# Grouped-query attention on one core: K transposed by DMA instead of on PE and DVE, with the order of work planned anew

## The chip, the core and the metric

One core of a Trainium2 chip. The time is that of one execution on the device in microseconds (us). Each execution also has a state: "slow" if it is more than 1.5% above the fastest of the same kernel. Comparisons here are between fast executions unless the text says otherwise.

PE is the matmul engine, PEld its weight load, DVE the vector engine, ACT the scalar engine (exponentials), POOL the general engine, SP the engine that issues most of the DMAs.

## The reference

```python
batch, seq, n_heads, n_kv_heads, dim = 8, 512, 32, 8, 64      # float32
# 4 Q heads share one K/V head; heads first, K and V repeated
scores  = einsum('bhqd,bhkd->bhqk', Q, K) * dim ** -0.5
weights = exp(scores - max(scores)); weights /= sum(weights) + 1e-10
output  = einsum('bhqk,bhkd->bhqd', weights, V)               # back to [b, s, h, d], float32
```

## The kernel before

The work is cut into 32 **units**: one batch times one pair of KV heads, with 8 Q heads. A unit has 16 **score tiles** of [128 keys, 2 heads, 512 queries]. PE writes a tile into one of three PSUM slots. Then 11 tiles go through `Exp` on ACT, and 5 through an exponential made of a multiply-add on DVE (two POOL operations refine one of the five).

```python
def mm_scores(t, slot):                      # a score tile: two 64-row matmuls
    s = spsum.tile([128, 2, S], FP32, name=f"s{slot}")
    ...
        nc.tensor.matmul(s[:, m, :],
            kt[u][64 * m:64 * m + 64, 0 if m == g else 1, kc * 128:(kc + 1) * 128],
            qt[u][64 * m:64 * m + 64, i, :], start=True, stop=True)
```

K and Q must be transposed to [dim, seq]. Both are loaded with a cast to bf16, transposed 128x128 at a time on PE and copied out of PSUM by DVE. K is wanted in two orientations (the pair's heads straight and swapped), and the swapped one is made by two DMAs:

```python
nc.vector.tensor_copy(out=k[:, 0, :], in_=x[:, 0:S])
nc.sync.dma_start(out=k[64:128, 1, :], in_=k[0:64, 0, :])
nc.sync.dma_start(out=k[0:64, 1, :], in_=k[64:128, 0, :])
```

PE's remaining work is cut into **fill pieces**: one output block (four 65-column matmuls, 0.12 us) or one 128x128 transpose (0.06 us). A class `Plan` works through a small timetable and from it fixes the order of instructions on every engine. Four strings and lists steer it: which tiles go to DVE, the order of ACT and DVE tiles, how many fill pieces follow each score tile, and the order of pieces. Each engine is given its instructions in that order.

```python
TILES  = [int(c) for c in "0100010001020100"]
SCORES = "ADAAADAADAADAADA"
FILL   = [0, 0, 8, 0, 0, 6, 9, 0, 0, 8, 0, 0, 12, 0, 0, 9]       # 52 pieces a unit
ORDER  = "K4 o6 o7 08 o7 18 o5 o7".split()                       # K4: four transposes of K
```

The softmax here doesn't subtract the row's maximum and nothing guards it: scores larger than these inputs give would overflow.

Of the kernel before, what the change touches and what calls it, by code (L numbers as in the profile page):

```python
# [10 lines left out]
FP32 = mybir.dt.float32  # L11
# [13 lines left out]
class Plan:  # L25
# [7 lines left out]
    def __init__(self, nu, kind, order, groups, arrive, x_cost, x_behind, fix, nslot, nx, npt):  # L33
# [3 lines left out]
        pt, pair_done, parts = {}, {}, {(0, None): 0.0, (0, 0): 0.0}  # L37
# [5 lines left out]
        carry = 0  # L43

        behind = 0.0

        def run_dve(until):
            nonlocal behind
            while ready:
                j = min(ready, key=lambda j: (max(j[0] - self.dve, 0.0), j[0]))  # L50
                start = max(self.dve, j[0])
                if start > until:
                    return
                ready.remove(j)
                self.ops.append((start, "dve", j[1], j[2]))
                extra = 0.0
                if j[1] != "turn":
                    extra, behind = behind, 0.0
                if j[1] == "score":
                    cost, vis = self.SCH, self.SCH_VIS  # L60
                    slots[j[3]] = start + vis
                    pt[j[2]] = start + vis + (fix if kind(j[2]) == 2 else 0.0)
                else:
                    cost, vis = x_cost(j[2])
                    xs[j[3]] = start + vis
                    if j[1] == "turn":
                        swap = 0.0 if j[2][2] is not None else 3.0 if j[2][1] == 1 else 6.0
                        parts[j[2][1:3]] = start + vis + swap
                    behind += x_behind(j[2])
                self.dve = start + cost + extra  # L70
# [11 lines left out]
        for u in range(nu + 3):  # L82
            scores, fill = order(min(u, nu - 1))
            for k in range(16):
# [32 lines left out]
                loose = u < 1 or u >= nu - 2  # L117
                while carry > 0 and gi < len(groups):
                    f = groups[gi]
                    if f[0] == "skip":  # L120
                        step = min(carry, f[1] - at)
                        carry, at = carry - step, at + step
                        if at == f[1]:
                            gi, at = gi + 1, 0
                        continue
# [30 lines left out]
                    carry -= 1  # L156
                    if at == 0 and f[0] != "close":
                        x = banks[f[2]] = nxt % nx
                        xs[x] = NEVER
                        nxt += 1  # L160
# [8 lines left out]
                carry = min(carry, 16)  # L169
# [6 lines left out]
def kernel(  # L176
# [21 lines left out]
    TILES = [int(c) for c in "0100010001020100"]  # L198
    SCORES = "ADAAADAADAADAADA"
    FILL = [0, 0, 8, 0, 0, 6, 9, 0, 0, 8, 0, 0, 12, 0, 0, 9]  # L200
    ORDER = "K4 o6 o7 08 o7 18 o5 o7".split()
    LAST_TILES = [int(c) for c in "0000200011010010"]
    LAST = {
        NU - 2: ("ADADAADAAAADADAA", [0, 0, 15, 32, 32, 0, 0, 0, 24, 0, 0, 0, 0, 0, 32, 3]),
        NU - 1: ("DAADAADDAAAADAAA", [1, 32, 0, 7, 1, 0, 7, 0, 0, 0, 0, 1, 0, 20, 32, 9]),
    }
    SKIP = 22
# [10 lines left out]
    kn_pool = ctx.enter_context(tc.tile_pool(name="kn", bufs=2))  # L218
# [3 lines left out]
    kt_pool = ctx.enter_context(tc.tile_pool(name="kt", bufs=4))  # L222
    pa_pool = ctx.enter_context(tc.tile_pool(name="pa", bufs=17))
    pd_pool = ctx.enter_context(tc.tile_pool(name="pd", bufs=7))
    lo_pool = ctx.enter_context(tc.tile_pool(name="lo", bufs=3))
    two_pool = ctx.enter_context(tc.tile_pool(name="two", bufs=2))
    raw_pool = ctx.enter_context(tc.tile_pool(name="raw", bufs=3))
# [5 lines left out]
    qn, kn, vn, v1 = {}, {}, {}, {}  # L233
    qt, kt = {}, {}
# [15 lines left out]
    def load_k(b):  # L250
        t = kn_pool.tile([128, SC, KV * D], BF16, name="k_nat")
        nc.gpsimd.dma_start(out=t, in_=rows(K, b, 0, KV))
        kn[b] = t
# [15 lines left out]
    def mm_scores(t, slot):  # L269
        p, kc = divmod(t, SC)  # L270
        u, i = divmod(p, HPG)
        s = spsum.tile([128, 2, S], FP32, name=f"s{slot}")
        g = 2 * i // HPG
        for m in range(2):
            nc.tensor.matmul(  # L275
                s[:, m, :],
                kt[u][64 * m:64 * m + 64, 0 if m == g else 1, kc * 128:(kc + 1) * 128],
                qt[u][64 * m:64 * m + 64, i, :],
                start=True,
                stop=True,  # L280
            )
        score[t] = s
# [15 lines left out]
    def exp_dve(t):  # L298
        two = tile_kind(t) == 2
        pts[t] = (two_pool if two else pd_pool).tile(  # L300
# [42 lines left out]
    def take_out(f, now):  # L343
# [6 lines left out]
        if last and lo >= 2 * BLK:  # L350
            divide(u, lo, n, nc.vector, x[:, 0:n * D1].rearrange("p (n c) -> p n c", c=D1))
            if lo == 2 * BLK + 4:
                store(u, 2 * BLK, BLK, nc.sync)
            elif lo >= 3 * BLK:
                store(u, lo, n, nc.scalar if lo == 3 * BLK else nc.sync)
            return
# [38 lines left out]
    def mm_turn(f, at):  # L395
        _, u, part, _ = f
        if at == 0:
            xs[f] = xpsum.tile([128, 2048], U8, name="x").bitcast(BF16)
        i, sc = divmod(at, SC)
        if part is None:  # L400
            src = kn[u // GP][:, sc, 128 * (u % GP):128 * (u % GP + 1)]
        else:
            j = 2 * part + i
            src = qn[u][:, sc, 128 * j:128 * (j + 1)]
        nc.tensor.transpose(xs[f][:, at * 128:(at + 1) * 128], src, ident)  # L405

    def take_turn(f):
        _, u, part, _ = f
        x = xs.pop(f)
        if part is None:  # L410
            k = kt_pool.tile([128, 2, S], BF16, name="kt")
# [3 lines left out]
            kt[u] = k  # L415
# [8 lines left out]
    def tile_kind(t):  # L424
        return (LAST_TILES if t >= 16 * (NU - 1) else TILES)[t % 16]

    turned = {}
    groups = [("skip", 2), ("turn", 0, 1, 8), ("skip", 4), ("turn", 1, None, 4)]
    groups += [("skip", SKIP - 6), ("turn", 1, 0, 8), ("turn", 1, 1, 8)]
    for u in range(NU - 1):  # L430
        lo = 0
        for word in ORDER:
            kind, n = word[0], int(word[1:])
            if kind == "o":
                groups.append(("out", u, lo, n))
                lo += n
            elif u + 2 < NU:
                groups.append(("turn", u + 2, None if kind == "K" else int(kind), n))
# [16 lines left out]
    def arrive(f):  # L455
        return {(0, 1): 0.5, (1, None): 3.0}.get(f[1:3], 6.0 if f[1] == 1 else 0.0)

    plan = Plan(
        NU, tile_kind, lambda u: LAST.get(u, (SCORES, FILL)), groups, arrive, x_cost, x_behind,
        fix=6.0, nslot=NSLOT, nx=2, npt=6,  # L460
    )

    with tc.manual_schedule(engines={PE, ACT, DVE, POOL, SP}):
        q32 = first.tile([128, SC, HPG * D], FP32, name="q32")
        k32 = first.tile([128, SC, 2 * D], FP32, name="k32")
        v32 = first.tile([128, SC, 2 * D], FP32, name="v32")
        q16 = first.tile([128, SC, HPG * D], BF16, name="q16")
        k16 = first.tile([128, SC, 2, 2 * D], BF16, name="k16")
        warm = first.tile([128, S], BF16, name="warm")
        nc.sync.dma_start(out=k32, in_=rows(K, 0, 0, 2))  # L470
        nc.scalar.dma_start(out=q32[:, :, 0:2 * D], in_=rows(Q, 0, 0, 2))
        nc.sync.dma_start(out=q32[:, :, 2 * D:4 * D], in_=rows(Q, 0, 2, 4))
# [10 lines left out]
        load_k(0)  # L483
        load_q(1)

# [4 lines left out]
        nc.vector.tensor_copy(out=k16[:, :, 0, :], in_=k32)  # L490
        nc.vector.tensor_copy(out=k16[:, :, 1, 0:D], in_=k32[:, :, D:2 * D])
        nc.vector.tensor_copy(out=k16[:, :, 1, D:2 * D], in_=k32[:, :, 0:D])
        nc.scalar.copy(out=q16[:, :, 0:2 * D], in_=q32[:, :, 0:2 * D])
        kt[0] = kt_pool.tile([128, 2, S], BF16, name="kt")
        qt[0] = qt_pool.tile([128, HPG, S], BF16, name="qt")

        def turn_first(src, copy, dst):
            x = xpsum.tile([128, 2048], U8, name="x").bitcast(BF16)
            for sc in range(SC):
                nc.tensor.transpose(x[:, sc * 128:(sc + 1) * 128], src[:, sc, :], ident)  # L500
            copy(out=dst, in_=x[:, 0:S])

        turn_first(k16[:, :, 0, :], nc.vector.tensor_copy, kt[0][:, 0, :])
        turn_first(q16[:, :, 0:2 * D], nc.scalar.copy, qt[0][:, 0, :])
        turn_first(k16[:, :, 1, :], nc.vector.tensor_copy, kt[0][:, 1, :])
        nc.vector.tensor_copy(out=q16[:, :, 2 * D:4 * D], in_=q32[:, :, 2 * D:4 * D])
# [3 lines left out]
        load_v(0)  # L510
# [3 lines left out]
        pending_first = True  # L514
        due = False
        for now, engine, what_kind, what in plan.ops:
# [6 lines left out]
            elif engine == "pe":  # L523
                b, r = divmod(what[0], 16 * GP)
                if r == 24 and b + 1 < B:
                    load_k(b + 1)
                    load_v(b + 1)
# [3 lines left out]
                if pending_first and what[0] > 0:  # L531
                    pending_first = False
                    turn_first(q16[:, :, 2 * D:4 * D], nc.vector.tensor_copy, qt[0][:, 1, :])
# [41 lines left out]
```

## Time and profile before

| | before |
|---|---|
| time, median | 350.9 us |
| span in the profile | 349.2 us |
| first exponential on ACT | 7.90 us |
| units 0 and 1 together | 20.76 us |
| a steady unit (median of units 6 to 28) | 10.34 us |
| last exponential to the end | 7.0 us |

The unit times are distances between starts of ACT's exponentials (every eleventh) in the trace's records. From the page of the kernel before: the busy time of each engine, then the chain of waits by engine and by line, then the two large DMA queues.

```profile
PE 336.7 (96%) x5774; PEld 224.5 (64%) x5774; DVE 329.1 (94%) x463; ACT 333.7 (96%) x356; POOL 280.2 (80%) x201
...
PE 48%; ACT 38%; POOL 5%; DVE 3%; issue 3%; DMA 1%; POOLq 0%; ACTq 0%
...
q0 software_dynamic: 25344, 24.91, 47.5%
q1 hardware_dynamic: 25552, 38.28, 32.3%
```

Three engines are at 94 to 96%, and no one of them holds the chain alone: PE has 48% of it, ACT 38%. The DMA queues have 80% of the engines' time.

The timeline of ACT in the kernel before. Columns: start, length, engine, line, operation, number; in brackets the idle time before it and its releaser. The first two lines are the start, the third is a piece from the middle.

```profile
7.90 10.19 ACT L288 ACTIVATE pa<-s 128x1024 bf16<-128x1024 f32 x11 [0.75 <-PE s L275]
18.32 15.95 ACT L288 ACTIVATE pa<-s 128x1024 bf16<-128x1024 f32 x17 [0.23 <-PE s L275]
...
79.42 100.60 ACT L288 ACTIVATE pa<-s 128x1024 bf16<-128x1024 f32 x107
```

The third line says "no idle for 100 us", yet the pace is readable: (100.60 - 1.02) / 106 = 0.939 us from start to start, while exponentials whose input is ready start 0.904 us apart. One exponential is 1.02 us long and the next starts 0.904 us after it, so the two overlap; a wait shorter than this overlap does not count as idle.

### The profile page before, as it was taken

Reading aid. Unit: us, or ns where it says so; the run is one execution under the profiler, and the core shown is the slowest. Engines: PE = TensorE matmul, PEld = TensorE weight load, DVE = VectorE, ACT = ScalarE, POOL = GpSimd, SP = SyncE. Lnnn points to the kernel's source line nnn. Section 1 sums busy time; section 2 is a strip of 40 time slices with the busy share of each in tenths; the row PEclk is TensorE's granted clock in tenths of the full one; section 3 lists DMA queues with packets and bytes.
Section 4 is the critical chain, followed back from the end, with each engine's and each line's share of the span. In section 5 each row is a group of like instructions: output and inputs, shape, how many; then the busy total and the mean of one; then the engine's idle time right before and its main releaser. Section 6 shows DMA issues by size and latency. Waiting matters only on the chain.

```text
span 349.2 us, 12952 instructions
## 1 busy us (share of the span) xinstructions
PE 336.7 (96%) x5774; PEld 224.5 (64%) x5774; DVE 329.1 (94%) x463; ACT 333.7 (96%) x356; POOL 280.2 (80%) x201
## 2 busy tenths in 40 slices
PE   8799999999999999999999999999999999999992
PEld 3366666666666666666666666666666666666661
DVE  3899999999999999999999999999999999999982
ACT  3999999999999999999999999999999999999981
POOL 6369797879978797987978889787997879787692
PEclk9999999999999999999999999999999999999997
DMA  8999567898669958698786986799765996823337
GB/s 184 208 156 181 160 174 196 192 203 200 164 161 237 263 115 207 141 237 222 196 198 140 215 198 168 194 198 224 170 171 163 234 259 129 208 86 137 122 141 223
DMA packets 52008, 64.40 MB, mean 184 GB/s; under 512 B 3441, under 2 KB 36593, under 8 KB 51953
## 3 DMA queue, kind: packets, MB, share of 16 engines
q0 software_dynamic: 25344, 24.91, 47.5%
q1 hardware_dynamic: 25552, 38.28, 32.3%
q8 instruction: 45, 0.74, 0.8%
q10 hardware_dynamic: 1056, 0.39, 0.4%
q14 instruction: 11, 0.08, 0.1%
HBM read 50.86 MB, written 33.55 MB: 242 GB/s over the span
## 4 chain that ended last, share of the span: by engine, by line
PE 48%; ACT 38%; POOL 5%; DVE 3%; issue 3%; DMA 1%; POOLq 0%; ACTq 0%
ACT pa L288 38%; PE s L275 21%; PE x L334 19%; PE x L405 6%; POOL o_sb L378 3%; DMA kt<-kt 1%; DVE pd L305 1%; PE x L488 1%; POOL sum L321 1%; POOL hi L315 1%; DVE raw L357 1%; DVE qt L419 1%; PE x L500 0%; DVE lo L305 0%; POOLq L570 0%
## 5 line engine op out<-in xcount | busy, mean ns | idle before, releaser
L288 ACT ACTIVATE pa<-s 128x1024 bf16<-128x1024 f32 x353 | 331.2, 1027 | 3.9 <-PE s L275 3.3
L275 PE MATMUL s<-qt,kt 64*128 64x512 bf16 x1024 | 163.1, 381 | 4.3 <-ACT pa L288 1.4
L305 DVE TENSOR_SCALAR pd<-s 128x1024 uint16<-128x1024 f32 x128 | 155.9, 1218 | 2.0 <-PE s L275 2.0
L334 PEld LDWEIGHTS <-pa 128*128 128x128 bf16 x2816 | 135.8, 97 | 29.2 <-issue 29.0
L334 PE MATMUL x<-v,pa 128*128 128x65 bf16 x2728 | 150.6, 194 | 0.2
L334 PE MATMUL x<-v,pd 128*128 128x65 bf16 x992 | 131.8, 194 | 0.2 <-DVE raw L357 0.2
L378 POOL TENSOR_TENSOR o_sb<-raw,inv 128x1024 f32<-128x1024 f32 (+1 forms) x64 | 118.7, 1880 | 1.7 <-DVE inv L373 1.3
L275 PEld LDWEIGHTS <-kt 64*128 64x128 bf16 x1024 | 55.8, 93 | 68.5 <-issue 37.8
L334 PEld LDWEIGHTS <-pd 128*128 128x128 bf16 x1024 | 98.8, 98 | 0.4 <-issue 0.2
L357 DVE COPY raw<-x 128x455 f32<-128x455 f32 (+3 forms) x159 | 91.8, 579 | 4.7 <-PE x L334 4.1
L315 POOL TENSOR_TENSOR hi<-lo,shift 128x512 int32<-128x512 int32 x32 | 40.6, 1268 | 49.3 <-PE x L334 37.6
L321 POOL TENSOR_TENSOR sum<-lo,hi 128x1024 bf16<-128x1024 bf16 x32 | 68.0, 2125 | 2.5
L405 PE MATMUL x<-ident,q_nat 128*128 128x128 bf16 x504 | 43.6, 220 | 0.0
L419 DVE COPY qt<-x 128x1024 bf16<-128x1024 bf16 x63 | 42.8, 680 | 0.0
L305 DVE TENSOR_SCALAR lo<-s 128x1024 uint16<-128x1024 f32 x32 | 39.1, 1222 | 0.5 <-PE s L275 0.5
L405 PEld LDWEIGHTS <-q_nat 128*128 128x128 bf16 x504 | 29.9, 98 | 7.7 <-issue 7.7
L334 PE MATMUL x<-v,sum 128*128 128x65 bf16 x248 | 34.7, 194 | 0.0
L245 POOL DMA_DIRECT2D q_nat<-in_Q_dram x32 | 25.5, 797 | 0.0
L334 PEld LDWEIGHTS <-sum 128*128 128x128 bf16 x256 | 25.0, 98 | 0.2 <-issue 0.2
L263 POOL COPY v<-v_nat 128x2048 bf16<-128x2048 bf16 x8 | 15.2, 1905 | 5.7 <-DMA v_nat<-in_V_dram 5.7
L405 PE MATMUL x<-ident,k_nat 128*128 128x128 bf16 x124 | 17.3, 222 | 0.0
L405 PEld LDWEIGHTS <-k_nat 128*128 128x128 bf16 x124 | 7.5, 98 | 7.1 <-issue 7.1
(35 smaller groups left out, 66.7 us busy)
## 6 DMA issues: line engine op xcount, KB each, us to landing
out_dram<-o_sb SPq DMA_DIRECT2D x30, 1024.0 KB, 5.3
q_nat<-in_Q_dram POOLq DMA_DIRECT2D x31, 512.0 KB, 5.9
k_nat<-in_K_dram POOLq DMA_DIRECT2D x8, 512.0 KB, 8.8
v_nat<-in_V_dram POOLq DMA_DIRECT2D x8, 512.0 KB, 10.8
kt<-kt SPq DMA_DIRECT2D x62, 64.0 KB, 5.1
out_dram<-o_sb SPq DMA_DIRECT2D x2, 512.0 KB, 3.8
out_dram<-o_sb SPq DMA_DIRECT2D x3, 256.0 KB, 3.9
q<-in_Q_dram ACTq DMA_DIRECT2D x1, 256.0 KB, 4.5
```

Source lines behind the costliest of these rows:

```text
L245: nc.gpsimd.dma_start(out=t[:, :, lo * D:], in_=rows(Q, b, HU * gp + lo, HU * (gp + 1)))
L263: nc.gpsimd.tensor_copy(out=t[:, :, :, 0:D], in_=vn.pop(b).rearrange("p sc (h d) -> p sc h d", h=KV))
L275: nc.tensor.matmul(s[:, m, :], kt[u][64 * m:64 * m + 64, 0 if m == g else 1, kc * 128:(kc + 1) * 128], qt[u][64 * m:64 * m + 64, i, :], st ...
L288: recent.append(nc.scalar.activation(out=pts[t][:, ms, :], in_=src[:, ms, :], func=mybir.ActivationFunctionType.Exp, scale=float(scale),))
L305: nc.vector.tensor_scalar(out=bits, in0=score.pop(t), scalar1=float(A_schr), scalar2=float(B_two if two else B_one), op0=mybir.AluOpType.mult,
L315: nc.gpsimd.tensor_tensor(out=high.rearrange("p m s -> p (m s)").bitcast(I32), in0=bits.rearrange("p m s -> p (m s)").bitcast(I32), in1=shift,
L321: nc.gpsimd.tensor_tensor(out=dst, in0=bits.bitcast(BF16), in1=high.bitcast(BF16), op=mybir.AluOpType.add)
L334: nc.tensor.matmul(xs[f][:, at * D1:(at + 1) * D1], pts[(u * HPG + i) * SC + kc][:, m, qc * 128:(qc + 1) * 128], v1[u][:, kc, 2 * i // HPG ...
L357: nc.vector.tensor_copy(out=raws[u][:, lo:lo + n, :], in_=x[:, 0:n * D1])
L378: eng.tensor_tensor(out=osbs[u].rearrange("p qc h d -> p h qc d")[:, lo // SC + h0:lo // SC + h0 + nh], in0=src[:, :, 0:D].rearrange("p (h ...
L405: nc.tensor.transpose(xs[f][:, at * 128:(at + 1) * 128], src, ident)
L419: nc.vector.tensor_copy(out=qt[u][:, 2 * part:2 * part + 2, :], in_=x)
```

## The change

Its intent: take K of batches 1 to 7 off PE and DVE. A casting DMA puts K as bf16 into DRAM, one DMA transpose brings a batch's K into SBUF, two DMAs make the swapped orientation. The freed time is to be used by a new order. The first tiles' loads are cut smaller. More output work is done in units 0 and 1, so that the end has less to catch up. The diff, cut to its core:

```diff
+    def load_k(b):
+        ks[b] = ks_pool.tile([S, KV * D + 64], BF16, name="ks")[:, 0:KV * D]        # DRAM
+        nc.gpsimd.dma_start(out=ks[b], in_=K[b].rearrange("s h d -> s (h d)"))
+    def turn_k(b):
+        straight[b] = kt_pool.tile([128, GP, S], BF16, name="straight")
+        nc.sync.dma_start_transpose(out=straight[b], in_=ks.pop(b))
+    def swap_k(b):
+        t = straight.pop(b)
+        k = kt_pool.tile([128, GP, S], BF16, name="swapped")
+        nc.sync.dma_start(out=k[0:64], in_=t[64:128])
+        nc.sync.dma_start(out=k[64:128], in_=t[0:64])
 ...
+    rank = {t: i - (early + 0.5 if kind(t) == 2 else 0.0) for i, t in enumerate(qd)}   # two-step tiles earlier
 ...
-    TILES = [int(c) for c in "0100010001020100"]
-    FILL = [0, 0, 8, 0, 0, 6, 9, 0, 0, 8, 0, 0, 12, 0, 0, 9]
-    ORDER = "K4 o6 o7 08 o7 18 o5 o7".split()
+    TILES = [int(c) for c in "0100020100010001"]
+    FILL = [0, 0, 7, 0, 0, 7, 0, 0, 7, 0, 0, 7, 0, 10, 0, 10]
+    ORDER = "o6 18 08 o7 o7 o7 o5".split()
+    ORDER_FIRST = "o7 K4 18 o5 08 o7 o7 o6".split()
+    EARLY = 3
+    HEAD = 114                                    # pieces done before unit 2; and own orders for 4 units
 ...
+    load, turn, swap = (24, 40, 52) if n == 1 else (64 * n - 80, 64 * n - 52, 64 * n - 26)   # tile numbers
 ...
-        nc.sync.dma_start(out=k32, in_=rows(K, 0, 0, 2))
-        nc.scalar.dma_start(out=q32[:, :, 0:2 * D], in_=rows(Q, 0, 0, 2))
-        nc.sync.dma_start(out=q32[:, :, 2 * D:4 * D], in_=rows(Q, 0, 2, 4))
+        nc.sync.dma_start(out=k32[:, 0:1], in_=rows(K, 0, 0, 2)[:, 0:1])
+        nc.scalar.dma_start(out=q32[:, 0:half], in_=rows(Q, 0, 0, 2)[:, 0:half])
+        nc.sync.dma_start(out=k32[:, 1:SC], in_=rows(K, 0, 0, 2)[:, 1:SC])
+        nc.scalar.dma_start(out=q32[:, half:SC], in_=rows(Q, 0, 0, 2)[:, half:SC])
+        nc.sync.dma_start(out=q32b, in_=rows(Q, 0, 2, 4))
```

## The prediction

> **What bounds the kernel now.** The page shows three engines full at once: PE 96%, ACT 96%, DVE 94% of 349.2 us. The starts of ACT's exponentials in the trace split this. From unit 1 to unit 29 (a unit is 16 score tiles, 11 on ACT, 5 on DVE) one unit takes 10.34 us. Back-to-back exponentials start 0.904 us apart, so ACT alone needs 11 x 0.905 = 9.96. (The Trainium skill, "ScalarE: Activation LUTs", section "What ACT_TABLE_LOAD costs", gives 186 + 0.833 x 1024 - 93 = 946 ns; the trace's 0.904 decides.) The other 0.38 us are waits of about 0.1, three or four a unit: pitches of 1.0 to 1.07 us, the exponential starting 0.04 after a score matmul ended. Summed start to start, DVE needs 5 x 1.141 (exponentials) + 2.58 (five output evictions) + 2 x 0.597 (Q) + 0.278 (K) + 0.26 (reciprocal) = 10.0. PE needs about 9.8: scores 16 x 0.222, outputs 32 x 0.123, 20 transposes x 0.057, some 0.1 per switch. All three lie within 5% of 10.34, coupled by three score slots; the coupling costs the rest.
>
> Outside the steady part: the first exponential starts at 7.90 us (K lands 4.8, Q 5.25, then cast, transposes, evictions); the last two units take 11.25 and 12.02, since PE then catches up on outputs that lag about a unit; the last exponential ends at 342.2, the last store 7.0 later.
>
> **What changes.** For batches 1 to 7, K's transposes leave PE (0.23 us a unit) and its eviction leaves DVE (0.278 a unit). They become a casting DRAM-to-DRAM load, a DMA transpose and two half-swaps a batch. DVE falls to 9.74, PE to about 9.6; ACT stays 9.96 and becomes the longest. Exponentials per unit stay 11 and 5. The first inputs are cut smaller; K's orientations for units 0 and 1 are made on chip. 114 fill pieces precede unit 2 (about 80 now), so outputs lag half a unit less and the tail has less to catch up.
>
> The transpose moves 512 KB a batch. The Trainium skill, "DMA: Bandwidth & Descriptors", section "Latency and other measured facts", gives 261 GB/s: an estimate of 2 us; no trace of before shows one. At least 24 tiles lie between its steps (12 for batch 1), so I expect it hidden.
>
> **Sum (estimates).**
> - Steady part: 10.34 to 10.07 (most of the coupling goes), 28 units: -7.6 us.
> - First exponential at 6.7: -1.2.
> - Units 0 and 1 carry more fills: +0.3.
> - Last two units 23.3 to 20.9: -2.4.
> - After the last exponential: -0.1.
>
> 350.9 - 11.0 = 339.9 us. Range 336.5 to 344.0. Faster by over 2% (below 343.9) 0.80, within 2% 0.17, slower 0.03.
>
> **What would show it.** Steady unit near 10.0 to 10.1, ACT at 98%, DVE idle about 3%; in the chain of waits ACT's exponential well over its 38%; fewer than one pitch over 1.0 us a unit; first exponential before 7 us; last two units under 10.6 each; PE transposes down by about 112, K evictions by 28.
>
> **What would make it wrong.** The steady unit stays above 10.2, because the score slots and not the sums set it. K of batch 1 lands late and PE stalls near 45 us. Transposes hold the sync queue and delay stores, or fill the DMA engines (already about 80% busy), so that Q lands late. Early fills starve ACT in the first two units.

## The result, and the profile after

Twelve executions of the changed kernel gave a median of 355.7 us, from 345.9 to 476.7. Eight were slow: six between 355.2 and 360.2 us, and two at 418.0 and 476.7 us. The four fast ones were 345.9 to 348.8 us, a ratio to the fast executions of before of 0.990 (interval 0.988 to 0.992). Fourteen executions of the kernel before in the same rounds were all within 350.6 to 351.4. A ratio here is the mean time of one kernel's fast executions over that of the other's in the same rounds, so it is not quite the ratio of the medians quoted.

The profile fell on the slowest execution. From its page: busy times, the clock granted to PE in 40 slices (tenths of full speed), and the chain of waits.

```profile
PE 467.7 (98%) x5666; PEld 277.4 (58%) x5666; DVE 331.3 (70%) x436; ACT 345.0 (73%) x356; POOL 280.8 (59%) x205
...
PEclk7555555555555555555555555555555555555555
...
PE 96%; DMA 2%; ACT 1%; POOL 0%; issue 0%; DVE 0%; POOLq 0%; DVEq 0%
```

PE had 0.555 of its clock from 4.15 us to 471.8 us and was the bound. This says nothing about the change's design. The same kernel was run again (a1_again), and its profile fell on a fast execution: busy times, chain, DMA queues.

```profile
PE 333.3 (97%) x5666; PEld 220.3 (64%) x5666; DVE 322.6 (94%) x436; ACT 329.8 (96%) x356; POOL 280.9 (82%) x205
...
ACT 66%; PE 22%; DVE 3%; issue 3%; DMA 2%; POOL 2%; DVEq 0%; POOLq 0%; ACTq 0%
...
q1 hardware_dynamic: 36080, 41.55, 45.4%
q0 software_dynamic: 25872, 24.78, 44.7%
```

ACT now holds 66% of the chain, as intended, and the DMA queues take 90% of the engines' time for 80% before. ACT's timeline of the same execution, the start and a piece from the middle:

```profile
7.39 1.94 ACT L310 ACTIVATE pa<-s 128x1024 bf16<-128x1024 f32 x2 [1.66 <-PE s L297]
9.95 1.02 ACT L310 ACTIVATE pa<-s 128x1024 bf16<-128x1024 f32 x1 [0.62 <-PE s L297]
11.30 6.60 ACT L310 ACTIVATE pa<-s 128x1024 bf16<-128x1024 f32 x7 [0.32 <-PE s L297]
18.63 1.94 ACT L310 ACTIVATE pa<-s 128x1024 bf16<-128x1024 f32 x2 [0.73 <-PE s L297]
21.16 1.94 ACT L310 ACTIVATE pa<-s 128x1024 bf16<-128x1024 f32 x2 [0.59 <-PE s L297]
23.32 1.94 ACT L310 ACTIVATE pa<-s 128x1024 bf16<-128x1024 f32 x2 [0.22 <-PE s L297]
25.61 8.85 ACT L310 ACTIVATE pa<-s 128x1024 bf16<-128x1024 f32 x9 [0.35 <-PE s L297]
...
79.79 101.14 ACT L310 ACTIVATE pa<-s 128x1024 bf16<-128x1024 f32 x109
```

In the middle the pace is (101.14 - 1.02) / 108 = 0.927 us for 0.939: better, but not 0.904. In the start ACT stops six times between 9 and 26 us where it stopped once before.

Where the time went, between the two fast traces (all from the starts of exponentials; the spans are 349.2 and 344.2 us):

| stretch | before | after, fast | difference | predicted |
|---|---|---|---|---|
| to the first exponential | 7.90 | 7.39 | -0.5 | -1.2 |
| units 0 and 1 | 20.76 | 24.09 | +3.3 | +0.3 |
| units 2 to 29 | 289.7 | 285.9 | -3.8 | -7.6 |
| units 30 and 31 | 23.9 | 22.1 | -1.8 | -2.4 |
| last exponential to the end | 7.0 | 4.7 | -2.3 | -0.1 |
| sum | 349.2 | 344.2 | -5.0 | -11.0 |

Two questions remain: why a fast execution is 6 us slower than predicted, and what the slow ones are.

### The profile page after: what moved, and what is told of

Read it like the earlier page. It is cut to its first block, busy times and chain, and to the rows that moved or that the text cites. A ratio compares the mean times of both kernels' runs of the same rounds, so it can differ in the third digit from the quotient of the medians.

```text
span 474.9 us, 12653 instructions
## 1 busy us (share of the span) xinstructions
PE 467.7 (98%) x5666; PEld 277.4 (58%) x5666; DVE 331.3 (70%) x436; ACT 345.0 (73%) x356; POOL 280.8 (59%) x205
## 4 chain that ended last, share of the span: by engine, by line
PE 96%; DMA 2%; ACT 1%; POOL 0%; issue 0%; DVE 0%; POOLq 0%; DVEq 0%
PE x L356 44%; PE s L297 42%; PE x L428 11%; DMA q_nat<-in_Q_dram 2%; ACT pa L310 1%; DVE o_sb L401 0%; DVE inv L396 0%; POOL shift L511 0%; POOL ident masks.py:199 0%; POOL ident masks.py:197 0%; POOL v1f L508 0%; POOLq masks.py:199 0%; DVEq L396 0%; POOLq L623 0%
## 5 line engine op out<-in xcount | busy, mean ns | idle before, releaser
L310 ACT ACTIVATE pa<-s 128x1024 bf16<-128x1024 f32 x353 | 342.9, 1019 | 121.4 <-PE s L297 121.1
L356 PEld LDWEIGHTS <-pa 128*128 128x128 bf16 x2816 | 188.7, 117 | 93.9 <-issue 93.2
L356 PE MATMUL x<-v,pa 128*128 128x65 bf16 x2728 | 207.6, 222 | 0.0
L356 PE MATMUL x<-v,pd 128*128 128x65 bf16 x992 | 192.2, 234 | 0.0
L297 PE MATMUL s<-qt,swapped 64*128 64x512 bf16 x448 | 188.3, 539 | 0.1
L297 PE MATMUL s<-qt,straight 64*128 64x512 bf16 x448 | 188.4, 536 | 0.0
L337 POOL TENSOR_TENSOR hi<-lo,shift 128x512 int32<-128x512 int32 x32 | 40.4, 1262 | 167.4 <-DVE lo L327 167.3
L356 PE MATMUL x<-v,sum 128*128 128x65 bf16 x248 | 49.3, 240 | 0.0
L297 PEld LDWEIGHTS <-swapped 64*128 64x128 bf16 x448 | 34.6, 106 | 21.8 <-issue 10.6
L297 PEld LDWEIGHTS <-straight 64*128 64x128 bf16 x448 | 34.5, 106 | 18.8 <-issue 6.4
L297 PE MATMUL s<-qt,kt 64*128 64x512 bf16 x96 | 21.5, 528 | 1.3 <-DVE qt L536 0.8
```

The source lines that it names most:

```text
L297: nc.tensor.matmul(s[:, m, :], kt[u][int(m != g) if u > 1 else g][64 * m:64 * m + 64, kc * 128:(kc + 1) * 128], qt[u][64 * m:64 * m + 64, ...
L310: recent.append(nc.scalar.activation(out=pts[t][:, ms, :], in_=src[:, ms, :], func=mybir.ActivationFunctionType.Exp, scale=float(scale),))
L337: nc.gpsimd.tensor_tensor(out=high.rearrange("p m s -> p (m s)").bitcast(I32), in0=bits.rearrange("p m s -> p (m s)").bitcast(I32), in1=shift,
L356: nc.tensor.matmul(xs[f][:, at * D1:(at + 1) * D1], pts[(u * HPG + i) * SC + kc][:, m, qc * 128:(qc + 1) * 128], v1[u][:, kc, 2 * i // HPG ...
```

## The experiments

Theories for the slow executions: **A**, the new start uses PE too thinly and the clock gate misbehaves; **B**, a limiter answers to the denser steady part; **C** and later **K**, the DMA transpose, or rather K of batch 1 coming late. For the steady unit: **E**, the sum of work on an engine sets it; **L**, a loop through ACT, a score slot and PE's in-order fill chunk sets it.

### First round: the kernel again, its two halves, a longer warm-up

a1_again: no edit.

> The changed kernel once more, to have a trace of a fast execution and more executions to count. Theory A (the start: the clock gate does not open cleanly with the new start) expects that slow executions differ from fast ones by the clock alone, from the first microseconds on, and that a fast one has steady units of about 10.05 to 10.2 us. Theory B (a limiter answers to the denser steady part) expects the granted clock to fall only once the steady part runs, in stretches in the middle. Fast executions about 346 us, slow ones 354 to 480, about half of all.

Measured: fast at 345.4 to 347.7 us (ratio 0.987, interval 0.985 to 0.989), 2 of 6 slow (355.3 and 355.5 us at clocks 0.989 and 0.982). The steady unit is 10.18 us.

a2_konly: the kernel before, with K by DMA and, from unit 3 on, four pieces fewer in the fill list. Core of the edit:

```diff
+    FILL2 = [0, 0, 7, 0, 0, 5, 8, 0, 0, 7, 0, 0, 12, 0, 0, 9]
-            elif u + 2 < NU:
+            elif u + 2 < (GP if kind == "K" else NU):
-                    load_k(b + 1)
+                    ...  # send_k, turn_k, swap_k at the changed kernel's tile numbers
```

> The kernel before with one part of the change alone: K of batches 1 to 7 by casting load, DMA transpose and swaps; start, tile order and tail as before. Theory A (start) expects every execution at full clock, as before, and a time of 347 to 349 us if the steady unit falls a little (PE and DVE have 0.25 us less per unit). Theory B (denser steady part) expects slow executions here too. If the DMA transpose itself costs, this is slower than before at full clock.

Measured: 363.3 us, **3.5% slower than before** (1.034 to 1.037), all four executions fast, clock 0.990 to 0.996. The steady unit rose from 10.34 to 10.70 us although PE and DVE have less to do. ACT's timeline in it:

```profile
86.93 10.49 ACT L311 ACTIVATE pa<-s 128x1024 bf16<-128x1024 f32 x11 [0.19 <-PE s L298]
97.62 10.52 ACT L311 ACTIVATE pa<-s 128x1024 bf16<-128x1024 f32 x11 [0.19 <-PE s L298]
```

The hoped-for 347 to 349 us did not come; of what was expected, only "slower than before at full clock" did, which would blame the DMA transpose. The changed kernel has the same transposes and a unit of 10.18 us, so they alone do not cost this. It is a first blow to theory E: work was removed and the unit grew. That my four removed pieces had shifted the rest against the score tiles is likely, but no run shows it by itself. K of batch 1 was in time here: 4.3 us before its first use in the trace.

a3_nokdma: the changed kernel, with K of batches 1 to 7 on PE again: `K4` in `ORDER`, and `FILL = [0, 0, 8, 0, 0, 8, 0, 0, 8, 0, 0, 8, 0, 10, 0, 10]`.

> The changed kernel with K of batches 1 to 7 turned on PE again (one 4-block group a unit, eviction on DVE, swaps by DMA); new start, orders and tail stay. Theory A (start) expects slow executions at low clock here as well, about as often; theory B (density from the freed PE and DVE) expects none. Fast executions: steady unit back at about 10.3 us, so 347 to 350 us.

Measured: 380.2 us (ratio 1.083), 5 of 5 fast, steady unit 11.42 us, not 10.3. The order that I gave it was bad, so it does not tell what K's work costs on PE. It has the changed kernel's start and no slow execution, which speaks against theory A, though its trace does have 3.4 us at half clock, from 9.5 us on.

a4_warm16: `for _ in range(16):` in place of 10.

> The changed kernel with 16 warm-up matmuls instead of 10: PE is busy without a break for about 7 us instead of 4.3. Theory A (start) expects the slow executions to become rare or vanish, with fast ones within 1.5 us of those of the changed kernel (first exponential up to 1.5 us later). Theory B expects slow executions as often as without.

Measured: 2 of 6 slow (354.4, 357.5 us); fast ones 345.5 to 348.1. Theory A falls back further. In its trace the first exponential came 1.6 us later than in a1_again, yet unit 2 began at 31.4 us as there (31.5): something later in units 0 and 1 than the first exponential sets their end.

### Second round: density, the transpose, the fill chunk, one load

b1_dense: seven 512-column matmuls around the transposes that wait for the second pair of Q heads.

```diff
                 if scored == 3:
+                    fill_pe(5)
                     turn_first_q(1)
+                    fill_pe(2)
```

> The changed kernel with seven idle-filling matmuls of 512 columns in the start, where PE waits for the second pair of Q heads. Theory A (PE is too thinly used in the first 15 us, and the clock gate[...] closes or opens late) expects slow executions to vanish (0 of about 6, where the changed kernel had 10 of 18), fast time within 1 us of the changed kernel's. Theory B (limiter answers to a dense steady part) and theory C (the DMA transpose or a late K) expect slow ones as often as before.

Measured: 1 of 4 slow (354.6 us). Theory A's cure doesn't cure.

b2_plain: the transpose replaced by a plain DMA; the result is wrong.

```diff
-        nc.sync.dma_start_transpose(out=straight[b], in_=ks.pop(b))
+        nc.sync.dma_start(out=straight[b], in_=ks.pop(b).rearrange("(g p) s -> p g s", p=128))
```

> The changed kernel with the DMA transpose replaced by a plain DMA of the same 512 KB into the same tile; the result is wrong on purpose. Theory C (transpose engages or delays something) expects no slow executions, and if the transpose burdens the steady part, a unit below 10.18 us. Theories A and B expect slow executions in about half of the runs and the same steady unit of 10.18 us: then the transpose is free.

Measured: 345.9 us, 4 of 4 fast, steady unit 10.18 us. The transpose burdens the steady part no more than a plain DMA of the same bytes. From issue to landing the plain DMA took 9.6 to 10.3 us, the transpose of the same 512 KB 9.9 to 11.6 us in a1_again. It is about as slow as the loads of its size here (median 7.9 to 10.6 us in a1_again), and not the estimated 2 us. The issues with their median time to landing, in a1_again and then in b2_plain, and PE's wait for the swapped K of batch 1 in b2_plain:

```profile
straight<-ks SPq DMA_TRANSPOSE x7, 10.7
...
straight<-ks SPq DMA_DIRECT2D x7, 512.0 KB, 10.1
...
PE s L297 <- DMA swapped<-straight: 0.3, 1, 0.3
```

So K of batch 1 was not in time here either, and its wait of 0.3 us cost little: unit 3 took 10.9 us. Four fast executions do not free the transpose of blame, nor do they convict it.

b3_detune: the same 48 pieces a unit, placed otherwise.

```diff
-    FILL = [0, 0, 7, 0, 0, 7, 0, 0, 7, 0, 0, 7, 0, 10, 0, 10]
+    FILL = [0, 0, 9, 0, 0, 6, 0, 0, 7, 0, 0, 6, 0, 10, 0, 10]
```

> The changed kernel with the same 48 fill pieces a unit in other places: 9, 6, 7, 6, 10, 10 between the scores instead of 7, 7, 7, 7, 10, 10. Not one instruction more or less. Theory L (the steady unit is a loop: an exponential ends, PE scores the freed slot, does the whole fill chunk, scores the next tile, whose exponential may then start) expects about 10.4 us a unit, some 7 us more in all; theory E (engine sums set it) expects 10.18. For the slow state: theory B (density of the steady part) expects none or few, as the unit is slower than before's 10.34; theory A expects about half.

Measured: 362.7 us, all at clocks of 0.974 to 0.984. The steady unit is 10.41 us. ACT's timeline:

```profile
106.98 10.24 ACT L310 ACTIVATE pa<-s 128x1024 bf16<-128x1024 f32 x11 [0.17 <-PE s L297]
117.40 10.23 ACT L310 ACTIVATE pa<-s 128x1024 bf16<-128x1024 f32 x11 [0.17 <-PE s L297]
127.80 10.23 ACT L310 ACTIVATE pa<-s 128x1024 bf16<-128x1024 f32 x11 [0.17 <-PE s L297]
```

Each unit of 11 exponentials now ends in a visible stop of 0.17 us, and the units start 10.42 and 10.40 us apart, with not one instruction more or less than the changed kernel. This agrees with theory L, which had said 10.4 (from the kernel's own timetable arithmetic), against theory E, which had said no change. The slower units are not the whole difference to a1_again: much of the rest is a single unit of 21.4 us, taken up in the third round. The low clocks of all five suggest that all have it; then all count as fast by the rule, though none is undisturbed.

b4_q32b: `nc.scalar.dma_start(out=q32b, ...)` for `nc.sync.dma_start(out=q32b, ...)`.

> The changed kernel with one line moved: the load of the second pair of Q heads is issued by ACT behind the first pair instead of third on the sync queue. It landed at 7.99 us and the first unit waited for it. Expected: lands near 6.5 to 7, units 0 and 1 together 23 us instead of 24.1, total 1 us less in fast executions; if theory A holds, somewhat fewer slow executions.

Measured: 348.1 us (ratio 0.991), worse. The load landed at 9.55 us, later than on the sync queue, where it landed between 5.4 and 8.2 us in the traces of nine runs; unit 0 took 14.9 us and the clock was at half for 6.8 us in it, from 10.6 us on. A miss: another issuing engine did not make this load faster. None of its 5 executions was slow. So half clock in the start, which theory A fears, does occur, but the execution with it took 348.1 us, not 354.

### Third round: K of batch 1

b3_detune's trace had shown, besides its slower unit, one unit of 21.4 us: PE waited 8.3 us for the swapped K of batch 1, since its order had put a store ahead of the swap on the sync queue, and the clock was at half for 10.2 us, from 4 us into that wait on. In the fast trace of the changed kernel the same data comes only just in time. The timeline of the sync queue in a1_again (start, time on the queue, line, what is moved), then in a second fence, from PE's timeline of the same execution, its first matmul on the swapped K of batch 1:

```profile
31.19 0.39 SPq L413 DMA_DIRECT2D out_dram<-o_sb  x1
31.68 5.73 SPq L267 DMA_TRANSPOSE straight<-ks  x1
41.61 0.47 SPq L272 DMA_DIRECT2D swapped<-straight  x1
42.13 0.59 SPq L273 DMA_DIRECT2D swapped<-straight  x1
45.96 0.40 SPq L413 DMA_DIRECT2D out_dram<-o_sb  x1
```

```profile
47.19 0.38 PE L297 MATMUL s<-qt,swapped 64*128 64x512 bf16 x1
```

The load lands at 31.58 us, the transpose at 41.60, the second swap at 45.84: a margin of 1.35 us. Right behind the swap comes a 1 MB store. If the chain were 2 us later, the swap would share the DMA engines with that store. First use is at 47.2 us, well before unit 4 begins (its first exponential is at 52.0), because `EARLY` pulls a two-step DVE tile forward.

c0_again: no edit, as the base on the same chip.

> The changed kernel once more, as the base on the same chip for the next three. Over all runs so far 10 of 18 were slow. Theory K (K of batch 1 is late: in fast traces its swapped half landed at 45.8 us and was first used at 47.2, a margin of 1.35 us, and right behind it the sync queue starts a 1 MB store) expects slow executions again, between one and four of six, about 8 to 9 us longer.

Measured: 2 of 6 slow (354.5, 358.0 us); the ratio of the fast ones is 0.988 (0.984 to 0.992).

c1_early: `(16, 32, 44) if n == 1` for `(24, 40, 52)`.

> The changed kernel with the chain of K of batch 1 (load, transpose, swap) issued 8 tiles earlier, one line. Theory K expects no slow execution in six and fast ones at the changed kernel's fast times (346 to 347), give or take 1 us for loads that compete in the start. Theories A (clock gate in the start by itself) and B (dense steady part) expect slow ones as often as in the base.

Measured: 345.7 us, 4 of 4 fast, ratio 0.985 (0.983 to 0.987). The load itself moved by only 0.4 us (POOL reached it at 22.8 us), but the transpose now stands before the store and landed at 38.2 us. Its swap then ran beside the end of the store (to 40.4 us) and a load of Q (to 45.8 us) and took 8.4 us, so the margin was 0.6 us in this trace, less than in a1_again, and unit 3 took 10.7 us for 10.2. No execution was slow, but four are few.

c2_late: `(27, 40, 52) if n == 1`.

> The same chain pushed the other way: the load of K of batch 1 issued 3 tiles (about 2 us) later, transpose and swap at the same places. Theory K expects every execution slow, 353 to 358 us, with a wait of PE for the swapped K of some 3 to 7 us near 47 us in the trace, the granted clock at half for one to three windows after it, and unit 3 at 18 to 20 us instead of 10.2. Theories A and B expect no change from the base.

Measured: 347.9 to 355.0 us, median 353.0. By the 1.5% rule three count as slow, but five of the six are at a clock of 0.989 or 0.990 and 351.6 us or more; one escaped. The load was issued at 34.4 us, 11 us later and not 2, because its place in POOL's order came after other work. From its trace, of a slow execution: the waits between 40 and 60 us (engine, line, releaser; total, times, longest), then PE and its clock in 40 slices.

```profile
ACT pa L310 <- PE s L297: 8.2, 2, 7.0
...
PE s L297 <- DMA swapped<-straight: 6.8, 1, 6.8
```

```profile
PE   7799938999999999999999999999999999999994
...
PEclk9999996999999999999999999999999999999999
```

PE waits 6.8 us for the swapped K (47.43 to 54.19). The granted clock is at half for 6.83 us (51.63 to 58.46), 4.3 us of it after the wait. Unit 3 takes 19.0 us for 10.2. The Trainium skill, "TensorE: Matmul & The Clock Gate", section "Part 1: The HAM clock gate (the "warmup" mystery)", says that the gate goes to half clock after an idle window of about 3.4 us. The traces agree in the lengths, 6.83 us here and 10.24 us in b3_detune, two and three times 3.413; and PE was idle for the whole 3.4 us before the drop in both. But a full window of idleness was not needed: in d2_best, below, PE was busy for 46% of the 3.4 us before the drop. So a late K costs its wait and then a stretch at half clock: 8.8 us in all here.

c3_split: transpose and swap of each batch cut in two, the first KV pair's quarter first.

```diff
+        nc.sync.dma_start_transpose(out=t[:, 0:1], in_=ks[b][:, 0:128])
+        nc.sync.dma_start(out=k[0:64, 0], in_=t[64:128, 0])
+        nc.sync.dma_start(out=k[64:128, 0], in_=t[0:64, 0])
+        nc.sync.dma_start_transpose(out=t[:, 1:GP], in_=ks.pop(b)[:, 128:])
```

> The changed kernel with each batch's transpose and swap cut in two: the first pair of KV heads (a quarter of the bytes) first, the other three behind it. Theory K expects K of the first unit of batch 1 to land at about 38 to 40 us, a margin of over 6 us, so no slow execution, and fast ones as in the base.

Measured: 346.2 us, 4 of 4 fast, within 0.5 us of each other, ratio 0.986 (0.985 to 0.988). The first quarter landed, swapped, at 41.1 us, later than the 38 to 40 expected, with a margin of 6.4 us.

### Fourth round: the start, and a better version

In c3_split's trace PE waits 0.8 us, until 19.7 us, for Q of unit 2, a load that POOL issues only at 11.9 us, after casts that wait for other loads.

d1_loadq: c3_split, with that load issued before the casts.

```diff
+        load_q(2)
         load_k_pairs(2, 2)
         load_v(0)
 ...
-        load_q(2)
         load_q(3)
```

> The split version (no slow executions) with one more line moved: the load of Q for unit 2 is issued by POOL before its casts of the first tile, which wait for other loads, instead of after them. In the split version it was issued at 11.9 us, landed at 19.7 and PE waited 0.8 us for it, and ACT with it. If the waits for Q set units 0 and 1 (12.6 and 12.1 us), unit 1 falls by 0.8 to 1.5 us and the total to about 345; if the larger number of fill pieces before unit 2 sets them, little changes.

Measured: units 0 and 1 fell from 24.8 to 23.6 us, but 3 of 6 executions were slow (351.9 to 358.4 us). The trace is a slow one: the first quarter's transpose, issued at 33.2 us, landed at 45.4, PE waited 5.7 us for the swapped K, unit 3 took 17.8 us and the clock was at half for 6.8 us. The sync queue and PE's wait:

```profile
30.52 0.40 SPq L420 DMA_DIRECT2D out_dram<-o_sb  x1
33.16 1.60 SPq L273 DMA_TRANSPOSE straight<-ks  x1
45.41 0.47 SPq L274 DMA_DIRECT2D swapped<-straight  x1
...
PE s L304 <- DMA swapped<-straight: 5.7, 1, 5.7
```

Splitting the chain did not make it safe: a quarter took 12 us here and 6 in c3_split. It was not the transpose alone: the store issued at 30.5 us took 11.8 us to land (6.2 in c3_split), and the load of Q at 33.9 us 11.7 (5.8). Why all transfers were slow at that time is not known.

d2_best: d1_loadq with measured arrivals in the timetable and other orders for units 0, 1 and the steady part.

> As the one before, with the order of work planned again for the loads' measured arrivals in the first two units, and a steady order of fill pieces and exponentials (fill 7, 7, 7, 7, 11, 9, other DVE tiles) that the loop theory puts at 10.13 us a unit for 10.17. Expected: steady unit 10.13 to 10.15, last two units 0.3 less, units 0 and 1 together 22.5 to 24, no slow execution, total 343 to 345 us, so faster than both kernels. If engine sums set the steady unit, it stays at 10.18 us.

Measured: 353.1 us (ratio 1.005), a failure in every point but one. The steady unit is 10.17 us, so the 10.13 that the loop account promised did not come; K was late twice in the trace (of the slowest execution, 356.3 us), by 2.4 us for the first KV pair and by 3.2 us for the second, with 6.8 us at half clock after that, so that units 3 and 4 took 12.9 and 16.0 us; unit 31 grew to 12.4 us because its order no longer fitted. Only the start was as expected (23.7 us).

f1_margin: d1_loadq and c1_early together.

> d1 (split chain, Q of unit 2 loaded earlier) with the transpose of batch 1 placed ahead of the store on the sync queue (chain 8 tiles earlier, as in c1). In d1 the quarter transpose was issued at 33.2 us right behind a 1 MB store and landed at 45.4, 12 us later, so K was late again. Theory K expects the transpose to land by 38 us, a margin of at least 4 us, no slow execution in six, and d1's better start kept: units 0 and 1 at 23.6 us, total 345 us.

Measured: **344.5 us**, 5 of 5 fast, ratio 0.983 (0.981 to 0.986), the lowest of all, though not clear of c1, c3 and f2, whose intervals overlap it. The first quarter was transposed at 37.7 us and swapped at 42.0, 4.2 us before its first use. ACT's start in it:

```profile
7.02 3.06 ACT L317 ACTIVATE pa<-s 128x1024 bf16<-128x1024 f32 x3 [1.15 <-PE s L304]
10.42 6.60 ACT L317 ACTIVATE pa<-s 128x1024 bf16<-128x1024 f32 x7 [0.34 <-PE s L304]
17.98 3.85 ACT L317 ACTIVATE pa<-s 128x1024 bf16<-128x1024 f32 x4 [0.97 <-PE s L304]
22.35 1.94 ACT L317 ACTIVATE pa<-s 128x1024 bf16<-128x1024 f32 x2 [0.52 <-PE s L304]
24.60 9.77 ACT L317 ACTIVATE pa<-s 128x1024 bf16<-128x1024 f32 x10 [0.31 <-PE s L304]
```

Four stops after the first exponential where the changed kernel has six. Units 0 and 1 take 23.45 us for 24.09.

f2_head: f1_margin, with the load of K of batch 1 right behind that of Q for unit 3.

> f1 with the load of K of batch 1 issued in the start, right behind the load of Q for unit 3 (about 13 us instead of 23 to 25). Theory K expects the first quarter of K to land by 34 us, a margin over 10 us, no slow execution; the fast time as f1, or up to 1 us more if this load delays Q of units 2 and 3.

Measured: 345.5 us, 4 of 4 fast, ratio 0.985 (0.984 to 0.987). Its first quarter landed at 34.3 us and was swapped at 40.0, 6.5 us before use (I had expected over 10).

## Why the prediction was wrong

Three steps failed. K of batch 1 was taken as hidden, and with K late the kernel has, as far as the runs show, a second, slower speed. For the fast executions, 6 us short of the prediction, the steady units gave 3.8 us for 7.6, and units 0 and 1 cost 3.3 us for 0.3.

The prediction named the failing case ("K of batch 1 lands late and PE stalls near 45 us") but its sum said "I expect it hidden", and the range had no room for it. The step that failed is the estimate of the chain: 2 us for a transpose that takes 9.9 to 11.6 us from issue to landing beside the other traffic, and 12 tiles counted as room, when the first use comes about 5 us before unit 4 begins. In the fast trace of a1_again the load took 7.9 us, the transpose 9.9 and the swaps 4.2 to the last landing: 22.2 us of the 23.5 between the issue of the load and the first use. The Trainium skill, "DMA: Bandwidth & Descriptors", section "Latency and other measured facts", has 261 GB/s; 512 KB in 9.9 to 11.6 us is 45 to 53 GB/s.

What the runs show: with the chain as the change has it, in the changed kernel and in a4, b1 and b4, 15 of 39 executions were slow; 13 of 37 without the two at 418 and 476.7 us, which are something else. In the versions that issue the chain earlier (c1, f1, f2, of which f1 and f2 split it as well) none of 13 was. With 13 in 37 as the chance, none of 13 would come about in 0.4% of cases (an estimate; c1 was run on the chip of c0, f1 and f2 on another without the changed kernel beside them). The versions that only split it are divided: none of 4 in c3, 3 of 6 in d1. Where K was late, on purpose (c2), by the store ahead of the swap (b3) or by accident (d1, d2), the trace shows the wait for the swapped K, half clock from that wait on, and a unit or two that are together 8 to 11 us longer. Theory A does not account for the slow executions, since warm-up and idle-filling matmuls left slow ones, and half clock in the start of b4 came with 348.1 us; nor theory B, since c1, c3, f1 and f2 have the same dense steady part.

Three things stay open. What makes the transfers late in some executions is not known. The margin in one trace does not rank the versions: c1 with 0.6 us and b2 with none had no slow execution in 4 each. And the mean clock of an execution does not tell a late K: 0.990 went with 347.4 us in the changed kernel and 345.8 us in d1, and 0.989 with 352.0 us in the kernel before, measured beside c2. So one link is inferred: no trace of an execution at 354 to 360 us of the changed kernel itself was caught.

The two executions at 418 and 476.7 us are something else. In the latter the clock was limited from 4.15 us on, before any K of batch 1 was loaded, and K came with 10 us to spare. No execution of another version showed it, and its cause stays open.

**The steady unit: 10.18 us, not 10.07.** This is a mis-sized term; the mechanism was right. ACT did become the longest (66% of the chain for 38%), and pitches over 1.0 us fell from 2.1 to 0.1 a unit. But I took the coupling for something that vanishes when the sums fall. In the fast trace of a1_again an exponential runs from 114.08 to 115.10 us; PE scores a tile into its slot from 115.16; the fill chunk of 28 matmuls starts at 115.47; the next score starts at 116.43 and ends at 116.82; its exponential starts at 116.87. That is three exponentials in 2.787 us, 0.929 each, where ACT alone needs 3 x 0.904 = 2.712. So ACT is busy without a gap that counts as idle and still paced by PE's order. b3_detune shows that placing counts: not one instruction more, the unit 0.23 us longer. a2_konly shows the other side: with work taken off PE and DVE and the order not planned anew, the unit was 0.36 us longer. That this one loop is the whole difference is not shown; d2_best, planned by the same account for 10.13, stayed at 10.17.

**Units 0 and 1: +3.3 us, not +0.3.** The failing step is "Units 0 and 1 carry more fills: +0.3". The work taken from the end was put where PE, in order, waits for loads (0.8 us for one Q in c3). One moved load gave back 1.2 us (d1 against c3, kept in f1). One trace each would not show that, but the four traces with it (d1, d2, f1, f2) have 23.45 to 23.67 us, and the seven without it and with the changed kernel's start 24.09 to 25.24. The rest, about 2 us, is not separated further: the added pieces and the remaining waits for Q, V and K loads both lie there.

**The first exponential**: 6.85 to 7.39 us in fast traces of the changed kernel for 6.7 predicted. **The end**: the last two units gained 1.8 us for 2.4, but the stretch after the last exponential gained 2.3 for 0.1; together better than predicted. Evictions of K fell by 28 as said, and matmuls and transposes on PE by 108 (112 said).

## What to carry to other kernels

When engines that feed each other through few buffers are all near full, add up the loop (operation, slot, in-order chunk, next operation) as well as each engine's work; in a2, where work was removed and the order not planned anew, the kernel became slower. When a transfer replaces on-chip work, take its time from issue to landing under the kernel's own traffic, and compare its landing with the first use in the reordered program, above all for the first batch. A transfer of 512 KB that takes 5.4 to 12.3 us in the traces here, with a margin of 1 to 2 us, made a kernel with two speeds, and half clock on PE enlarged the miss; before asking what a limiter does, look for a wait of PE ahead of the drop (2.4 us in b4, 3.2 in d2, 5.7 to 8.3 in d1, c2 and b3; only in the start of a3 was none over 0.8).

## What the Trainium skill lacked or had wrong

- "DMA: Bandwidth & Descriptors", section "Latency and other measured facts": 261 GB/s for a transpose is no guide to its time beside other traffic. Here 512 KB took 9.9 to 11.6 us from issue to landing (45 to 53 GB/s), and a quarter of that 6 to 12 us for batch 1, with the DMA queues at 90%.
- "Advanced Engine Details and Errata", section "X-Bar Transpose (TRN2)", is not wrong here: it says that transposes are as fast as regular DMAs, and the runs agree: a plain DMA of the same bytes took 9.6 to 10.3 us.
- "TensorE: Matmul & The Clock Gate", section "Part 1: The HAM clock gate (the "warmup" mystery)", says that the K of the gate's events is 4 or 8 of 8 only, with 13/16 as a third state when three cores of a die are busy. One execution here, on one core, was granted 0.555 from 4.15 us to 471.8 us. Half clock for two or three windows of 3.413 us is as the page says, but its "idle window" is too narrow: by the traces PE was busy for 0% of the 3.4 us before the drop in c2 and b3, 26% in d1, 29% in b4, 46% in d2 and 57% in a3.
- "ScalarE: Activation LUTs", section "What ACT_TABLE_LOAD costs": an estimate from its figures is 186 + 853 - 93 = 946 ns between exponentials of 1024 columns; the traces have 903 to 904 ns when the input is ready and 920 ns right after one that had waited. No page has the second figure.
